# First products of the out-projection put into a chunk's last Strassen tile, side products later, zero products gone, stores by pairs

## The chip, the cores and the metric

The kernel runs on one core of one Trainium2 chip. The metric is device time in microseconds (us) from the first to the last instruction of a run; lower is better. Engine names are those of the profile: PE (TensorE matmuls), PEld (its weight loads), DVE (VectorE), ACT (ScalarE), POOL (GpSimd) and SP (SyncE, which issues most DMAs). A line number such as L751 is a line of the kernel before.

## The reference, cut to what matters

A decoder trunk of two layers over 512 tokens and 16 meta tokens, width 1024, all in float32. Each layer is FFN, token mixer, FFN, and each of these is wrapped in two RMSNorms:

```python
h = h + 0.5 * rmsnorm(swiglu(rmsnorm(h, g[0]), w_ffn_in[layer, 0], w_ffn_out[layer, 0]), g[1])
hn = rmsnorm(h, g[2])
mix = gla_mixer(...) if layer < 1 else swa_mixer(...)   # gated linear attention, then sliding-window attention
h = h + rmsnorm(mix, g[3])
h = h + 0.5 * rmsnorm(swiglu(rmsnorm(h, g[4]), w_ffn_in[layer, 1], w_ffn_out[layer, 1]), g[5])

def swiglu(x, w_in, w_out):
    gate, up = jnp.split(x @ w_in, 2, axis=-1)          # 2 x 2816 columns
    return (jax.nn.silu(gate) * up) @ w_out
```

So there are four FFNs. Between the layers one shared key/value set is computed. The output is `h` without the meta tokens.

## The kernel before, in words

**Numbers.** Every float32 factor of a large product is split into a high and a low part in a format that PE runs fast (`float32r`), and a product is three matmuls: high by high, low by high, high by low (`mm3s`, L333). ACT makes the high part (a copy) and DVE the low part (a subtraction), for activations and for weights alike; weights are split as they arrive (`split_part` L224, `split_pair` L236).

**An FFN** (`ffn`, L604) has 22 hidden tiles of 128, in chunks of 4, 6, 6 and 6 (`FF_CHUNKS`). A chunk makes its hidden tiles and then runs its part of the out-projection, which adds into `Y`. The first chunk (`ci == 0`) uses plain products: `x_first` (L509) multiplies two groups of tokens (the second, `gi == 1`, waits for less of the norm), then `x_units` (L486). Where a group has at most 256 columns, `x_first` puts two results into one bank of PSUM, and clears the bank first with a matmul of zeros by zeros over 512 columns. During that chunk `right_factors` (L666) prepares the right factors of the Strassen products on ACT and DVE.

The other three chunks of an FFN, 12 in all, go by `Strassen` (L711). A tile has seven products of 12 matmuls: `head` (11), `body` (s1, s2, 12, s3) and `tail` (s4, 22). Between them ACT and DVE copy and add. What matters here is in `body`:

```python
self.product(t.a, t, "s2", "t2", False)
act.activation(t.u2, t.a, AF.Copy)                  # L751
self.product(self.d, t, "12", "21", False)
act.activation(t.g1, self.d, AF.Silu)
self.product(t.a, t, "s3", "t3", False)             # adds to t.a, so it waits for L751
```

For all but the last tile, the head of the next tile stands between body and tail. After the tail, `gated` (L769) makes the hidden tile: a gate product on DVE (L770, L771), the high part on ACT (L774) and the low part on DVE (L775). The hidden tile of a tile is therefore finished while PE is already in the body of the next one.

**The out-projection** (`out_proj`, L552) has a unit for each of 8 output tiles `m` and each group of tokens: six hidden tiles by three matmuls, into one bank, which DVE adds to `Y` (L572). Groups are 272 and 256 columns wide in layer 0 and 512 in layer 1; in the last chunk of an FFN the units go by the two halves (`split_groups`), so that the norm of the first half can start early. `flow.wait(*jobs)` ahead of it makes sure that the instructions of all `gated` jobs have been emitted.

**Norms.** Sums of squares are made on ACT and POOL; PE adds them over partitions (`st_` matmuls), a chain of small instructions on DVE or POOL takes the inverse root (`rstd`, L348), and PE spreads the result over partitions (`r_` matmuls).

**What sets the order.** Each engine runs its instructions in the order in which the Python program emits them. The main loops emit PE's matmuls; side work (splits, norms, attention cores) is a generator in `Flow` (L60). Every matmul moves `flow.clock` on by its estimated time, and `flow.pump` runs those generators whose time has come; a `yield` of a number puts the rest off by so much, so an `st_` or `r_` matmul comes into PE's order a set time after the work that it needs was emitted. PE waits wherever that time was too short. Weights are loaded and split ahead under a budget (`set_ahead`, `prefetch` L300, `cap`).

**The end.** `Residual.store` (L471) adds the last residual by pairs of tiles, DVE and POOL, and stores each tile with a DMA of its own from SP.

Of the kernel before, what the change touches and what calls it, by code (L numbers as in the profile page):

```python
# [43 lines left out]
SCORE = 0.8  # L44
STAGGER = 5.0
SOFT = 5.0
NORM = 3.0
LAG = 3
NEG = -1e30
# [74 lines left out]
def trunk_kernel(ctx: ExitStack, tc, a, out):  # L124
# [19 lines left out]
    def ps(name):  # L144
        return pp.tile([P, 512], F32, tag="ps", name=name)
# [184 lines left out]
        released[0] += n  # L330


    def mm3s(outs, j, x, g, start, stop, shared=False):  # L333
        t, n = g
        cols = slice(j % 4 * P, (j % 4 + 1) * P)
        xh, xl = x[:, 0, t : t + n], x[:, 1, t : t + n]
        for o, w in outs:
            mm(o, w[j // 4][:, 0, cols], xh, start and not shared, False)
            mm(o, w[j // 4][:, 1, cols], xh, False, False)
        for i, (o, w) in enumerate(outs):  # L340
            mm(o, w[j // 4][:, 0, cols], xl, False, stop and (not shared or i % 2 == 1))
            flow.pump()

    def mm3(o, w, j, x, g, start, stop):
        mm3s([(o, w)], j, x, g, start, stop)


    def rstd(sq, n, dim, half, name, eng=pool):  # L348
        c = 128 if n % 128 == 0 else n // 4
        nch = n // c  # L350
        st = ps(f"st_{name}")
        for j in range(nch):
            for i, t in enumerate(sq):
                mm(st[:c, j : j + 1], t[:, j * c : (j + 1) * c], ones[:, 0:1], i == 0, i == len(sq) - 1)
        av = sm.tile([P, 4], F32, tag="av", name=f"av_{name}")
        yv = sm.tile([P, 4], F32, tag="yv", name=f"yv_{name}")
        zv = sm.tile([P, 4], F32, tag="zv", name=f"zv_{name}")
        wv = sm.tile([P, 4], F32, tag="wv", name=f"wv_{name}")
        aa, yy, zz, ww = av[:c, :nch], yv[:c, :nch], zv[:c, :nch], wv[:c, :nch]
        if eng is dve:  # L360
            dve.tensor_scalar(aa, st[:c, :nch], 1.0 / dim, 1e-6, op0=ALU.mult, op1=ALU.add)
        else:
            act.activation(aa, st[:c, :nch], AF.Identity, scale=1.0 / dim, bias=eps[:c])
        eng.tensor_scalar(yy.bitcast(I32), aa.bitcast(I32), -0.5, RSQRT_MAGIC, op0=ALU.mult, op1=ALU.add)

        eng.tensor_tensor(zz, yy, yy, op=ALU.mult)
        eng.tensor_tensor(zz, zz, aa, op=ALU.mult)
        eng.tensor_scalar(ww, zz, 0.375, -1.25, op0=ALU.mult, op1=ALU.add)
        eng.tensor_tensor(ww, ww, zz, op=ALU.mult)
        if eng is dve:  # L370
            dve.scalar_tensor_tensor(yy, ww, 1.875, yy, op0=ALU.add, op1=ALU.mult)
            dve.tensor_tensor(zz, yy, yy, op=ALU.mult)
# [10 lines left out]
        eng.tensor_tensor(  # L383
            dg[:c, :n].rearrange("p (j c) -> p j c", c=c),
            (hident if half else ident)[:c, :c].unsqueeze(1).to_broadcast([c, nch, c]),
            yy.unsqueeze(2).to_broadcast([c, nch, c]),
            op=ALU.mult,
        )
        yield DCHAIN if eng is dve else CHAIN
        r = ps(f"r_{name}")  # L390
        mm(r[:, :n], ones[:c, :], dg[:c, :n])
        return r
# [17 lines left out]
    class Operand:  # L410
# [25 lines left out]
        def factors(self, gi, eng=pool):  # L436
# [1 line left out]
                self.rt = sm.tile([P, TOK], F32, tag="R", name=f"R_{self.name}", bufs=2)  # L438
            o, n = self.groups[gi]
            yield FACT  # L440
            r = yield from rstd(self.accs[gi], n, D, False, f"{self.name}_{o}", eng)
            act.activation(self.rt[:, o : o + n], r[:, :n], AF.Copy)

        def need(self, gi, k):
# [3 lines left out]
    class Residual:  # L448
# [4 lines left out]
        def run(self, gi, g, sums):  # L453
# [7 lines left out]
            for k in range(KD):  # L461
# [4 lines left out]
                nxt.build(gi, k)  # L466
                nxt.sumsq(gi, k)
                yield 1.0
            nxt.rjob[gi] = flow.spawn(nxt.factors(gi))

        def store(self, gi, g, r):  # L471
            o, n = g
            rb = r[:, :n].unsqueeze(1).to_broadcast([P, 2, n])
            for k in range(0, KD, 2):
# [3 lines left out]
                t = t.rearrange("p (k n) -> p k n", n=n)  # L478
                dve.tensor_tensor(t, y, rb, op=ALU.mult)
                (pool if last else dve).tensor_tensor(h, t, h, op=ALU.add)  # L480
                for j in (k, k + 1):
                    sp.dma_start(out[j, :, o - META : o - META + n], H[:, j, o : o + n])
                yield 1.0


# [23 lines left out]
    def x_first(x, nu, evac, opening=False, behind=(), first_ahead=8):  # L509
# [13 lines left out]
        for gi, some in order + [(1, both)]:  # L523
# [4 lines left out]
            shared = n <= 256  # L528
            if shared:
                banks = [ps(f"x{used[0]}_{i}_{gi}") for i in some[::2]]  # L530
                for b in banks:
                    mm(b.rearrange("p (a c) -> p a c", c=P), zeros, zeros.unsqueeze(1).to_broadcast([P, 4, P]), True, False)
                pst = [banks[i // 2][:, i % 2 * 256 : i % 2 * 256 + n] for i in range(len(some))]
            else:
                pst = [ps(f"x{used[0]}_{i}_{gi}")[:, :n] for i in some]
# [13 lines left out]

    def out_proj(hid, groups, split_groups, first, finish=None, tailm=0, packed=False):  # L552
        nh = len(hid)
        ws = []

        def tile_of(m, j):
# [2 lines left out]
                ws.append(next_w())  # L559
            return ws[i], c  # L560

        def unit(m, g):
            o, n = g
            p = ps(f"y{used[0]}_{m}_{o}")
            for j, t in enumerate(hid):
                w, c = tile_of(m, j)
                mm3(p[:, :n], w, c, t, g, j == 0, j == nh - 1)
            y = Y[:, m, o : o + n]
            if first:
                act.activation(y, p[:, :n], AF.Copy)  # L570
# [12 lines left out]
            return (m + 1) * nh // 8 if packed else m + 1  # L583

        freed = 0
        for m in range(KD - tailm):
            for g in groups:
                unit(m, g)
# [15 lines left out]
    def ffn(x, groups, finish, opening=False, tail=4):  # L604
# [31 lines left out]
        for ci, (lo, hi) in enumerate(FF_CHUNKS):  # L636
# [9 lines left out]
            else:  # L646
# [2 lines left out]
                tiles = Strassen(z, halves)  # L649
                cur = tiles.head(new_hid())  # L650
                while cur:
                    tiles.body(cur)
                    nxt = tiles.head(new_hid()) if len(hids) < hi - lo else None
                    jobs.append(tiles.tail(cur, nxt is None))
                    cur = nxt
            flow.wait(*jobs)
            if lo < LAST:
                out_proj(hids, groups, x.groups, ci == 0)
            else:
                set_ahead(32)  # L660
                cap[0] = min(used[0] + NLAST + tail, len(units))
                out_proj(hids, groups, x.groups, False, finish, KD, True)

# [47 lines left out]
    class Strassen:  # L711
# [32 lines left out]
            act.activation(self.d, t.a, AF.Copy)  # L744
            return t

        def body(self, t):
# [3 lines left out]
            act.activation(t.u2, t.a, AF.Copy)  # L751
# [30 lines left out]
    def gla(x, finish):  # L782
        set_ahead(10)
        with tc.tile_pool(name="gp", bufs=1) as gp:
# [61 lines left out]
            def core(h, before):  # L846
# [516 lines left out]
```

## Time and profile before

| | |
|---|---|
| time, median of 3 runs (range) | 1956.11 us (1955.54 to 1958.57) |
| time of the profiled execution | 1955.57 us |
| span of its trace | 1953.7 us |
| PE busy | 1893.7 us, 97% |
| PEld, DVE, ACT, POOL busy | 92%, 73%, 51%, 11% |
| DMA moved | 174.63 MB, mean 89 GB/s |

The span runs from the first to the last instruction. "Busy" of PE counts modelled ends of pipelined matmuls, so PE's real pace is read from the starts: the time of a run of equal matmuls, divided by their number. In the list of waits a row names the waiting engine, the tile that it writes and its line, then what released it, and then the sum, the number of times and the longest, in us. In a table of windows each engine's busy time stands with its number of instructions in brackets, and PEclk is the granted TensorE clock as a share of full speed.

### The profile page before, as it was taken

Reading aid. Unit: us, or ns where it says so; the run is one execution under the profiler, and the core shown is the slowest. Engines: PE = TensorE matmul, PEld = TensorE weight load, DVE = VectorE, ACT = ScalarE, POOL = GpSimd, SP = SyncE. Lnnn points to the kernel's source line nnn. Section 1 sums busy time; section 2 is a strip of 40 time slices with the busy share of each in tenths; the row PEclk is TensorE's granted clock in tenths of the full one; section 3 lists DMA queues with packets and bytes.
Section 4 is the critical chain, followed back from the end, with each engine's and each line's share of the span. In section 5 each row is a group of like instructions: output and inputs, shape, how many; then the busy total and the mean of one; then the engine's idle time right before and its main releaser. Section 6 shows DMA issues by size and latency. Waiting matters only on the chain.

```text
span 1953.7 us, 37401 instructions
## 1 busy us (share of the span) xinstructions
PE 1893.7 (97%) x14522; PEld 1802.5 (92%) x14522; DVE 1420.8 (73%) x2868; ACT 1002.2 (51%) x2268; POOL 214.9 (11%) x417
## 2 busy tenths in 40 slices
PE   8999999999999999999999999999998999999997
PEld 7999999999999999999999898989976898989897
DVE  7885858665464788585887776768779779858584
ACT  5663636653235555353574453535636665636363
POOL 2000000221121400000024000000252140000002
PEclk9999999999999999999999999999999999999999
DMA  4332333322113122333251123232411212333331
GB/s 161 96 102 90 102 94 108 110 66 65 55 45 119 55 71 86 104 90 106 93 172 50 55 89 117 82 114 93 136 57 42 72 49 71 98 102 109 97 109 44
DMA packets 102145, 174.63 MB, mean 89 GB/s; under 512 B 11472, under 2 KB 24272, under 8 KB 101968
## 3 DMA queue, kind: packets, MB, share of 16 engines
q1 hardware_dynamic: 101680, 172.11, 28.3%
q8 instruction: 114, 1.87, 0.4%
q14 instruction: 63, 0.52, 0.1%
q10 hardware_dynamic: 288, 0.13, 0.0%
HBM read 170.10 MB, written 2.10 MB: 88 GB/s over the span
## 4 chain that ended last, share of the span: by engine, by line
PE 71%; DVE 20%; ACT 6%; issue 3%; POOL 0%; DMA 0%; SPq 0%; DVEq 0%; ACTq 0%
PE y L162 30%; PE x L162 16%; PE a L162 11%; DVE raw L251 4%; PE c L162 4%; DVE w_s L246 3%; DVE w L246 3%; ACT w_s L245 3%; PE d L162 3%; DVE w L227 2%; PE o L162 1%; PE e L162 1%; PE po L162 1%; ACT w L226 1%; DVE hidl0f L775 1%
## 5 line engine op out<-in xcount | busy, mean ns | idle before, releaser
L246 DVE TENSOR_TENSOR w_s<-raw,w_s 128x512 fp32r<-128x512 f32 x288 | 194.0, 690 | 134.6 <-ACT w_s L245 132.4
L227 DVE TENSOR_TENSOR w<-raw,w 128x512 fp32r<-128x512 f32 x378 | 244.0, 671 | 34.3 <-ACT w L226 32.4
L162 PE MATMUL y<-hidl0f,w 128*128 128x256 f32 (+1 forms) x2112 | 261.7, 285 | 1.3 <-DVE hidl0f L408 0.5
L162 PEld LDWEIGHTS y<-hidl0f,w 128*128 128x128 f32 x2112 | 258.8, 188 | 3.0 <-DVE hidl0f L408 1.0
L162 PE MATMUL y<-hidl1f,w 128*128 128x512 f32 (+1 forms) x1344 | 251.1, 346 | 1.5 <-ACT hidl1f L407 1.0
L245 ACT ACTIVATE w_s<-raw 128x512 fp32r<-128x512 f32 x288 | 175.4, 628 | 146.5 <-DVE raw L251 143.2
L162 PEld LDWEIGHTS y<-hidl1f,w 128*128 128x128 f32 x1344 | 212.3, 188 | 37.8 <-ACT hidl1f L407 1.8
L226 ACT ACTIVATE w<-raw 128x512 fp32r<-128x512 f32 x378 | 209.2, 586 | 51.3 <-PE y L162 41.8
L403 POOL TENSOR_TENSOR acc_post<-acc_post,sq_post 128x256 f32<-128x256 f32 (+1 forms) x72 | 57.0, 791 | 1408.8 <-ACT sq_post L402 1408.6
L251 DVE TENSOR_TENSOR raw<-raw,raw 128x512 f32<-128x512 f32 x288 | 197.9, 687 | 5.5
L246 DVE TENSOR_TENSOR w<-raw,w 128x512 fp32r<-128x512 f32 x216 | 148.2, 687 | 41.1 <-ACT w L245 40.2
L162 PE MATMUL x<-x_l0m,w 128*128 128x272 f32 (+1 forms) x1200 | 159.9, 290 | 0.0
L245 ACT ACTIVATE w<-raw 128x512 fp32r<-128x512 f32 x216 | 133.8, 621 | 47.9 <-PE y L162 47.6
L162 PEld LDWEIGHTS x<-x_l0m,w 128*128 128x128 f32 x1200 | 150.9, 190 | 1.2
L572 DVE TENSOR_TENSOR Y<-y,Y 128x256 f32<-128x256 f32 (+2 forms) x176 | 83.2, 473 | 80.7 <-PE y L162 80.2
L162 PE MATMUL a<-zl0f_t,w_s 128*128 128x264 f32 x864 | 118.7, 287 | 8.5 <-ACT c L751 8.5
L162 PE MATMUL a<-zl1f_t,w_s 128*128 128x256 f32 x864 | 115.1, 282 | 8.7 <-ACT c L751 8.4
L162 PEld LDWEIGHTS a<-zl0f_t,w_s 128*128 128x128 f32 x864 | 110.9, 190 | 9.8 <-ACT c L751 9.8
L162 PEld LDWEIGHTS a<-zl1f_t,w_s 128*128 128x128 f32 x864 | 107.0, 188 | 11.1 <-ACT c L751 11.1
L162 PE MATMUL x<-x_l0f,w 128*128 128x256 f32 (+1 forms) x768 | 102.2, 293 | 7.3 <-ACT w L226 6.4
L162 PEld LDWEIGHTS x<-x_l0f,w 128*128 128x128 f32 x768 | 98.7, 195 | 8.9 <-ACT w L226 6.7
L162 PE MATMUL x<-x_l1f,w 128*128 128x256 f32 (+1 forms) x576 | 93.2, 320 | 0.5 <-DVE x_l1f L426 0.5
(485 smaller groups left out, 3299.6 us busy)
## 6 DMA issues: line engine op xcount, KB each, us to landing
raw<-in_w_in SPq DMA_DIRECT2D x352, 256.0 KB, 2.9
raw<-in_w_out SPq DMA_DIRECT2D x96, 256.0 KB, 3.5
raw<-in_gla_in SPq DMA_DIRECT2D x50, 256.0 KB, 3.1
raw<-in_w_last SPq DMA_DIRECT2D x48, 256.0 KB, 3.1
raw<-in_w_out SPq DMA_DIRECT2D x64, 128.0 KB, 3.0
raw<-in_gla_out SPq DMA_DIRECT2D x16, 256.0 KB, 2.7
raw<-in_w_q SPq DMA_DIRECT2D x16, 256.0 KB, 3.9
raw<-in_swa_out SPq DMA_DIRECT2D x16, 256.0 KB, 2.7
```

Source lines behind the costliest of these rows:

```text
L162: inst = pe.matmul(o, lhs, rhs, start=start, stop=stop, skip_group_check=onto)
L226: act.activation(w[:, 0, :m], raw[:, :m], AF.Copy)
L227: dve.tensor_tensor(w[:, 1, :m], raw[:, :m], w[:, 0, :m].bitcast(F32), op=ALU.subtract)
L245: act.activation(w[:, 0, :512], src, AF.Copy)
L246: dve.tensor_tensor(w[:, 1, :512], src, w[:, 0, :512].bitcast(F32), op=ALU.subtract)
L251: dve.tensor_tensor(dst, dst, src, op=ALU.add)
L403: pool.tensor_tensor(sums[0][:, :n], sums[0][:, :n], t[:, :n], op=ALU.add)
L572: dve.tensor_tensor(y, p[:, :n], y, op=ALU.add)
L775: dve.scalar_tensor_tensor(t.hid[:, 1, g], t.h, -1.0, t.hid[:, 0, g].bitcast(F32), op0=ALU.mult, op1=ALU.subtract)
```

## The change

1. `out_proj` is now a generator, `out_steps`, behind a wrapper of the old name. A unit can be begun early: `begin(m, g)` does the products with all hidden tiles but the last, and `unit` later adds the last one. In a Strassen chunk the first unit is begun inside the last tile's body, between the product `12` and the product `s3` (`between`); after the tail, one further unit (512 columns) or two (256 and 272) are begun before `flow.wait(*jobs)`.
2. `BEHIND = 2.2` is added to the put-off times of some side products: the second group's `st_` (spawn of `factors`) and, in the opening, its `r_`; the transposes of the first attention core (`STATE_KEYS`); the `r_` of the last core's norm in `gla` (`h // 3`).
3. `x_first` has no zero matmuls: the first product of a shared bank has `start`, and those of the second half of the bank have not. That is 2 matmuls fewer in each of the first stages of the FFNs and mixers with two groups of 272 and 256 columns, 4 fewer where both groups have 256; 20 in all.
4. `store` issues one DMA for a pair of tiles, and two of the last four go from ACT instead of SP.

```diff
+BEHIND = 2.2
@@ mm3s
-        for o, w in outs:
-            mm(o, w[j // 4][:, 0, cols], xh, start and not shared, False)
-            mm(o, w[j // 4][:, 1, cols], xh, False, False)
         for i, (o, w) in enumerate(outs):
-            mm(o, w[j // 4][:, 0, cols], xl, False, stop and (not shared or i % 2 == 1))
+            second = shared and i % 2 == 1
+            mm(o, w[j // 4][:, 0, cols], xh, start and not second, False, second)
+            mm(o, w[j // 4][:, 1, cols], xh, False, False, second)
+        for i, (o, w) in enumerate(outs):
+            second = shared and i % 2 == 1
+            mm(o, w[j // 4][:, 0, cols], xl, False, stop, second)
             flow.pump()
@@ rstd(..., more=0.0)
-        yield DCHAIN if eng is dve else CHAIN
+        yield (DCHAIN if eng is dve else CHAIN) + more
@@ Operand.factors
-            r = yield from rstd(self.accs[gi], n, D, False, f"{self.name}_{o}", eng)
+            r = yield from rstd(self.accs[gi], n, D, False, f"{self.name}_{o}", eng, gi * BEHIND if eng is dve else 0.0)
@@ Residual.run
-            nxt.rjob[gi] = flow.spawn(nxt.factors(gi))
+            nxt.rjob[gi] = flow.spawn(nxt.factors(gi), gi * BEHIND)
@@ Residual.store
-                for j in (k, k + 1):
-                    sp.dma_start(out[j, :, o - META : o - META + n], H[:, j, o : o + n])
+                to = out[k : k + 2, :, o - META : o - META + n].rearrange("k p n -> p k n")
+                (act if gi and k % 4 else sp).dma_start(to, h)
@@ x_first
-                for b in banks:
-                    mm(b.rearrange("p (a c) -> p a c", c=P), zeros, zeros.unsqueeze(1).to_broadcast([P, 4, P]), True, False)
@@ out_proj
-    def out_proj(hid, groups, split_groups, first, finish=None, tailm=0, packed=False):
+    def out_proj(*args, **named):
+        for _ in out_steps(*args, **named):
+            pass
+
+    def out_steps(hid, groups, split_groups, first, finish=None, tailm=0, packed=False, jobs=()):
...
+        begun = {}
+
+        def begin(m, g):
+            o, n = g
+            p = begun[m, o] = ps(f"y{used[0]}_{m}_{o}")
+            for j, t in enumerate(hid[:-1]):
+                w, c = tile_of(m, j)
+                mm3(p[:, :n], w, c, t, g, j == 0, False)
+
         def unit(m, g):
             o, n = g
-            p = ps(f"y{used[0]}_{m}_{o}")
-            for j, t in enumerate(hid):
-                w, c = tile_of(m, j)
-                mm3(p[:, :n], w, c, t, g, j == 0, j == nh - 1)
+            if (m, o) not in begun:
+                begin(m, g)
+            p = begun[m, o]
+            w, c = tile_of(m, nh - 1)
+            mm3(p[:, :n], w, c, hid[-1], g, nh == 1, True)
...
+        if jobs:
+            order = [(m, g) for m in range(KD - tailm) for g in groups]
+            order += [(m, split_groups[0]) for m in range(KD - tailm, KD)]
+            begin(*order[0])
+            yield
+            for m, g in order[1 : 2 if order[1][1][1] == SEQ else 3]:
+                begin(m, g)
+            flow.wait(*jobs)
@@ ffn, a Strassen chunk
-                    tiles.body(cur)
-                    nxt = tiles.head(new_hid()) if len(hids) < hi - lo else None
-                    jobs.append(tiles.tail(cur, nxt is None))
+                    last = len(hids) == hi - lo
+                    if last:
+                        fin = (finish, KD, True) if lo >= LAST else (None, 0, False)
+                        proj = out_steps(hids, groups, x.groups, False, *fin, jobs)
+                        end = used[0] + NLAST + tail
+                    tiles.body(cur, (lambda: next(proj)) if last else (lambda: None))
+                    nxt = None if last else tiles.head(new_hid())
+                    jobs.append(tiles.tail(cur, last))
                     cur = nxt
...
+            for _ in proj:
+                pass
@@ Strassen.body(t, between)
             self.product(self.d, t, "12", "21", False)
             act.activation(t.g1, self.d, AF.Silu)
+            between()
             self.product(t.a, t, "s3", "t3", False)
@@ gla, core and its norm
-                yield STATE_KEYS
+                yield STATE_KEYS + (0 if h else BEHIND)
...
-                    r = yield from rstd(accs[gi], n, 256, True, f"go{h}_{gi}")
+                    r = yield from rstd(accs[gi], n, 256, True, f"go{h}_{gi}", more=h // 3 * BEHIND)
```

More of the change, by code (lines that the diff above doesn't have):

```diff
@@ L345, in mm3, with rstd @@
         mm3s([(o, w)], j, x, g, start, stop)
-    def rstd(sq, n, dim, half, name, eng=pool):
+    def rstd(sq, n, dim, half, name, eng=pool, more=0.0):
         c = 128 if n % 128 == 0 else n // 4
@@ L651, in ffn @@
                 while cur:
-                    tiles.body(cur)
-                    nxt = tiles.head(new_hid()) if len(hids) < hi - lo else None
-                    jobs.append(tiles.tail(cur, nxt is None))
-                    cur = nxt
[L656 to L659, printed above, removed]
+                    last = len(hids) == hi - lo
[6 more added lines that the diff above has]
+                    jobs.append(tiles.tail(cur, last))
+                    cur = nxt
+            if ci == 0:
+                flow.wait(*jobs)
+                out_proj(hids, groups, x.groups, True)
+                continue
+            if lo >= LAST:
                 set_ahead(32)
-                cap[0] = min(used[0] + NLAST + tail, len(units))
-                out_proj(hids, groups, x.groups, False, finish, KD, True)
+                cap[0] = min(end, len(units))
+            for _ in proj:
+                pass
     def right_factors(x, halves, z, plain):
@@ L745, in head, with body @@
             return t
-        def body(self, t):
+        def body(self, t, between):
             self.product(t.c, t, "s1", "t1", True)
```

## The prediction

> **What bounds the kernel now.** I read the page's chain and its groups first, then the list of PE's waits, then the stretches around them.
>
> ```profile
> PE 71%; DVE 20%; ACT 6%; issue 3%; POOL 0%; DMA 0%; SPq 0%; DVEq 0%; ACTq 0%
> ...
> L227 DVE TENSOR_TENSOR w<-raw,w 128x512 fp32r<-128x512 f32 x378 | 244.0, 671 | 34.3 <-ACT w L226 32.4
> ```
>
> PE carries 71% of the chain that ends last, DVE and ACT 26%, DMA nothing; the second row gives the price of a weight split on DVE, 0.67 us. So time is to be had where PE waits for DVE or ACT, or where it does needless matmuls. The waits:
>
> ```profile
> PE a L162 <- ACT c L751: 16.9, 12, 1.8
> ...
> PE pk L174 <- DVE f L880: 2.1, 1, 2.1
> PE st_l0f L162 <- ACT acc_l0f L399: 2.0, 1, 2.0
> PE r_l0f L162 <- DVE dg_l0f L383: 1.6, 2, 1.3
> PE r_go L162 <- POOL dg_go L383: 1.6, 1, 1.6
> ...
> PE st_l1m L162 <- POOL acc_l1m L403: 1.1, 1, 1.1
> PE st_kv L162 <- ACT acc_kv L399: 1.1, 1, 1.1
> PE st_l1m L162 <- ACT acc_l1m L399: 1.0, 1, 1.0
> ```
>
> The first row has 12 waits, as many as there are Strassen chunks. They are the s3 product of each chunk's last tile. The second chunk shows it (the last number of the second row is the wait):
>
> ```profile
> 143.23 1.61 PE L162 MATMUL d<-zl0f,w 128*128 128x264 f32 x12
> 146.10 1.74 PE L162 MATMUL a<-zl0f_t,w_s 128*128 128x264 f32 x12 [1.26 <-ACT c L751]
> ...
> 150.62 3.57 PE L162 MATMUL y<-hidl0f,w 128*128 128x272 f32 x27
> ```
>
> The copy it waits for comes late because ACT's order puts the hidden tile of the tile before (L774) ahead of it, and that waits for DVE:
>
> ```profile
> 144.33 0.65 ACT L774 ACTIVATE hidl0f<-c 128x528 fp32r<-128x528 f32 x1 [0.76 <-DVE c L771]
> ...
> 145.67 0.38 ACT L751 ACTIVATE c<-a 128x264 f32<-128x264 f32 x1
> ```
>
> The pace of PE comes from long runs of equal matmuls in the chain in order of time:
>
> ```profile
> 150.78 35.27 PE y L162 x288
> ...
> 1190.90 30.31 PE y L162 x129
> ```
>
> That is 0.122 us for 272 or 256 columns (35.27/288) and 0.235 us for 512 (30.31/129).
>
> **1. Products put into the last tile.** In the order of instructions of the changed program, 15 matmuls (five hidden tiles by three) move from the start of the out-projection to the place between the d product and s3; none is added. ACT's order around L751 stays. The d product's 12 matmuls take 12 x 0.122 = 1.46 us from 143.23, to 144.69, so PE really stands still for 1.41 us before 146.10, where the row says 1.26 (it lets a matmul end later). With 0.14 us more for each, the 12 waits are 16.9 + 1.7 = 18.6 us. The cover is 15 x 0.122 = 1.83 us, or 15 x 0.235 = 3.53 us in layer 1's 512-column chunks; the longest wait is 1.8 + 0.14 = 1.94 us.
>
> The products bring a wait of their own: the last three need the hidden tile of the tile before, the low part (L775) at the fifteenth matmul. Here are that instruction in this chunk and in the last one, with the product that follows:
>
> ```profile
> 145.01 0.71 DVE L775 SCALAR_TENSOR_TENSOR hidl0f<-c,hidl0f 128x528 fp32r<-128x528 f32 x1
> ```
>
> ```profile
> 1898.48 0.68 DVE L775 SCALAR_TENSOR_TENSOR hidl1f<-c,hidl1f 128x512 fp32r<-128x512 f32 x1
> ...
> 1899.16 1.69 PE L162 MATMUL a<-zl1f_t,w_s 128*128 128x256 f32 x12 [1.72 <-ACT c L751]
> ```
>
> In the first it is done at 145.72, and the fifteenth matmul starts at 144.69 + 14 x 0.122 = 146.40: no wait. In the last chunk the d product ends at 1899.16 - 1.72 - 0.14 = 1897.30, the fifteenth would start at 1899.01, and L775 ends at 1899.16. I leave 0.25 us there, and the same in the last chunk of each of the other FFNs, which end like it: 4 x 0.25 = 1.0 us. Queued behind these products in PE's order are s3, s4 and 22 and so the last hidden tile; s3 starts up to 3.53 - 1.41 = 2.1 us later than now in the 512-column chunks. DVE's addition behind s3 (L755) holds weight splits behind it by as much; the out-projection's first weights are split ahead of it, since the d product's own weights are later in DVE's order.
>
> After the tail PE has 30 begun matmuls as cover (3.7 us), or 15 of 512 columns (3.5 us), where it now has 15. The hidden tile is late by less than that today: PE goes from 150.62 through the first 15 without a wait that the list shows. I take nothing for it.
>
> **2. The clock.** Stretches of lower granted clock stand right behind waits that the change goes for. The longest wait for L751, and a table of windows (PEclk is the third column from the end):
>
> ```profile
> 343.31 2.72 PE L162 MATMUL a<-zl0f_t,w_s 128*128 128x264 f32 x12 [1.80 <-ACT c L751]
> ```
>
> ```profile
> 343.70:347.10 3.40, 3.40 (x18) 3.40 (x17) 2.63 (x6) 2.43 (x6) 0.00 (x0) 0.50 0.88 254
> 347.10:350.50 3.40, 3.40 (x30) 3.40 (x29) 2.40 (x5) 0.58 (x2) 0.00 (x0) 1.00 0.78 248
> 442.70:446.10 3.40, 3.40 (x18) 3.40 (x17) 2.00 (x5) 3.17 (x7) 0.00 (x0) 0.50 0.32 89
> 674.80:678.20 3.40, 3.40 (x19) 3.40 (x17) 1.86 (x4) 1.04 (x2) 2.65 (x9) 0.50 0.83 216
> 1899.20:1902.60 3.40, 3.40 (x29) 3.40 (x30) 3.33 (x7) 2.89 (x6) 0.00 (x0) 1.00 0.65 214
> ```
>
> The three at 0.50 follow the 1.8 us wait for L751, the 2.1 us for `pk` and the 2.0 us for `st_l0f`. Each does 18 or 19 matmuls where a full stretch does 30: 11 or 12 x 3.4/30, 1.3 us. With the waits I let them go: 1.3 us in part 1 and 2.6 us in part 3. The Trainium skill, in "TensorE: Matmul & The Clock Gate", Part 1, has the array fall to half rate after an idle window of about 3.4 us, and its closing table warns of gaps over about 3 us. By that rule these waits would cost no clock and the sum below would be 3.9 us smaller. The trace disagrees: half clock begins here behind waits of 1.8 to 2.1 us, so I go by the rows.
>
> Part 1 is thus 18.6 - 1.0 + 1.3 = **18.9 us** (bounds 0, if the wait for L775 took its place, and 19.9).
>
> **3. Side products later, and no zeros.** The 20 zero matmuls over 512 columns are 20 x 0.235 = 4.7 us of PE. `BEHIND` moves an `st_` or `r_` 2.2 us by the program's clock, about the size of each wait. But what follows an `st_` (the inverse root, the scaling by DVE) starts no earlier in real time. PE gets ahead and keeps the gain only if DVE isn't the bound up to PE's next need of it:
>
> ```profile
> 40.00:65.00 25.00, 24.53 (x196) 24.06 (x196) 23.75 (x49) 11.52 (x26) 0.00 (x0) 1.00 0.22 64
> 674.00:705.00 31.00, 30.48 (x235) 29.98 (x234) 24.84 (x51) 11.56 (x28) 3.84 (x12) 0.94 0.24 69
> 1052.00:1105.00 53.00, 52.50 (x339) 47.35 (x338) 37.87 (x79) 17.54 (x36) 7.62 (x16) 1.00 0.16 50
> 1441.00:1490.00 49.00, 42.09 (x246) 28.85 (x246) 41.11 (x116) 26.38 (x105) 19.15 (x28) 0.97 0.20 65
> ```
>
> DVE is the third engine in each row (PE, PEld, DVE, ACT, POOL): 95%, 80%, 71% and 84% busy. By stage, gross and what I keep:
>
> - First FFN: `r_l0f` 1.6 and 2 zeros 0.5 = 2.1. DVE is busy 23.75 of 25 us up to the hidden tile that the out-projection needs; its order has one right-factor instruction fewer ahead of it, about a weight split's 0.67 us. Kept 0.5.
> - GLA: 2 zeros 0.5, `pk` 2.1, its clock 1.3, `r_go` 1.6 = 5.5; PE bounds this stage. Kept 5.1.
> - Second FFN: 2.0, clock 1.3, 2 zeros 0.5 = 3.8. DVE's order has four right-factor instructions fewer ahead of the last hidden tile, 4 x 0.67 = 2.7 us. Kept 2.6.
> - Key/value and third FFN: `st_kv` 1.1 and 6 zeros 1.4 = 2.5; DVE has room. Kept 2.2.
> - Sliding-window attention: `st_l1m` 2.1 and 4 zeros 0.9 = 3.0. DVE bounds the softmax stretch, and 12 projection matmuls that fill PE's waits there now come earlier. Kept 1.2, between a loss of those 12 x 0.235 = 2.8 and a gain of 3.0.
> - Fourth FFN: 4 zeros 0.9. Kept 0.5.
>
> Gross 17.8, kept **12.1 us**.
>
> **4. Stores.** The last eight stores are issued over 4 us:
>
> ```profile
> 1947.32 4.01 SPq L482 DMA_DIRECT2D out<-H  x8
> 1947.66 1.28 DVE L480 TENSOR_TENSOR H<-t_out,H 128x512 f32<-128x512 f32 x2
> ```
>
> The last sum is ready at 1948.94 and the last issue ends at 1951.33. Four issues on two queues could save half of these 2.4 us, or nothing if the transfers themselves take the time; no row shows a 256 KB store. I take **0.6 us**, the middle of 0 and 1.2. What is queued on ACT behind them is nothing.
>
> **Sum:** 18.9 + 12.1 + 0.6 = 31.6 us off the profiled execution's 1955.57 gives 1924.0; the median of the runs is 0.5 us above that execution, so **1924.5 us**.
>
> **The rivals.**
>
> - *All of it is kept* (DVE's slack suffices everywhere, no wait left in part 1): 19.9 + 17.8 + 1.2 = 38.9 us, 1917.2. For it: DVE has 5 to 29% of room in the four stretches. Against: 23.75 of 25. Chance 0.12.
> - *DVE takes the side gains*: only GLA's 5.1 stays, and attention loses 2.8: 18.9 + 2.3 + 0.6 = 21.8 us, 1934.3. For it: the 95% and the 84%. Against: fewer right-factor instructions ahead of the hidden tiles. 0.15.
> - *Half-clock stretches come at other places*, behind waits that stay: 3.9 us less, 1928.4. For it: the 1.72 us wait at 1899.16 has none behind it (last row of that table), 1.8 us has, so place decides too. 0.10. By the rule of the Trainium skill's "TensorE: Matmul & The Clock Gate", Part 1, the time would be this one as well.
> - *It doesn't do what it says*: the products in the tile wait for L775 as long as s3 does for L751, part 1 is 0: 12.7 us, 1943.4. Against: L775 at 145.72. 0.03.
> - *Slower*: s3's delay is passed to DVE through L755, and out-projection splits of 0.67 us each come ahead of the last hidden tile, so that it outlasts the units begun. From 31.6/12 = 2.6 us, four splits, in each chunk it decides; with six (4.0 us) the kernel is 12 x 4.0 - 31.6 = 16.4 us slower, 1956.1 + 16.4 = 1972.5. Against: DVE's order has no split moved there. 0.04.
>
> The forecast itself (1919 to 1928) has 0.56.
>
> **How the numbers follow.** Range 1915 to 1936: it holds the forecast, the first three rivals but for their ends, about 0.85. A measurement of this kernel tells about 0.2%, 4 us, from no change. Faster by more than that: all cases but the slower one, 0.96, less 0.02 for mixtures of the last two that end near zero; so 0.94, 0.02 within, 0.04 slower.
>
> **What would show it.** Right: the row of waits for L751 falls from 12 times to at most the few of 0.2 us; `y` rows stand between d and s3; `st_l0f`, `st_l1m`, `st_kv`, `pk`, `r_go` are gone from the list; half-clock stretches at most one before the end; 20 matmuls fewer. Wrong: a row of `y` waiting for L775 or L774 of over 2 us in all, a wait of `y` for the plain chunk's hidden tiles (L407, L408) that grows by what `st_` and `r_` gave up, or longer waits of `ptm` and `sc` in attention.

## The result, and the profile after

| | before | changed |
|---|---|---|
| median of 4 runs each, same chip (range) | 1957.34 us (1955.54 to 1959.47) | 1932.53 us (1931.28 to 1935.86) |
| profiled execution, its span | 1955.57, 1953.7 us | 1932.53, 1930.5 us |
| PE instructions | 14522 | 14502 |

The ratio is 0.9875, with a 95% interval of 0.9858 to 0.9893: 24.8 us faster by the medians, 23.2 us by the spans of the two profiles, where 31.6 were forecast. The time is 8 us above the forecast and inside its range. That agreement is in part luck: it hides two errors of opposite sign, 4.2 and 12.6 us, as the stages will show.

In the changed kernel lines from L162 on lie further down: matmuls are L163, the copy L751 is L784, the low part L775 is L809, L407 and L408 are L411 and L412. First its chain of work and its list of PE's waits (sum, times, longest, in us):

```profile
PE 82%; DVE 12%; ACT 3%; issue 2%; POOL 1%; DMA 0%; SPq 0%; DVEq 0%; ACTq 0%
```

```profile
...
PE ptm L175 <- DVE mt L1169: 5.3, 2, 3.5
PE r_go L163 <- POOL dg_go L387: 4.1, 3, 2.4
PE y L163 <- ACT hidl0f L411: 3.1, 2, 2.5
...
PE o L163 <- DVE pt L1190: 1.7, 1, 1.7
...
PE x L163 <- ACT x_l1m L429: 1.3, 1, 1.3
PE o L163 <- DVE pt L1191: 1.1, 1, 1.1
...
PE x L163 <- DVE x_l1m L430: 0.6, 1, 0.6
...
PE a L163 <- ACT c L784: 0.2, 1, 0.2
```

PE's share of the chain rose from 71 to 82%: the last row, 16.9 us in 12 waits before, is nearly empty. `st_l0f`, `st_l1m`, `st_kv` and `pk` are gone from the list. In their place stand waits that were not there or were smaller: `r_go` 4.1 (from 1.6), `y` for the plain hidden tiles 3.1 (from 0.5), `x` for `x_l1m` 1.9 and `o` for `pt` 2.8 (neither stood in the list of before). The second chunk's last tile shows the first gain; the fifteen `y` matmuls stand between d and s3, and nothing waits:

```profile
144.84 1.62 PE L163 MATMUL d<-zl0f,w 128*128 128x264 f32 x12
146.29 2.05 PE L163 MATMUL y<-hidl0f,w 128*128 128x272 f32 x15
148.18 1.63 PE L163 MATMUL a<-zl0f_t,w_s 128*128 128x264 f32 x12
```

The next table is what the study rests on. It cuts each profile at the start of a matmul that every kernel has (the first of a Strassen chunk, the first `st_post_` of a stage) and gives the length of each stretch, for other kernels as the difference from before. In brackets stand the half-clock stretches of 3.413 us that begin in it. The kernels are described with their runs below; "again" is a second profile of the changed kernel.

| stretch | forecast | before | changed | again | p1_only | behind0 | best | between_only | ahead_only |
|---|---|---|---|---|---|---|---|---|---|
| up to the first chunk | -0.5 | 87.40 (0) | +1.74 (2) | -1.10 (0) | -0.03 (0) | -1.73 (0) | -0.09 (1) | -0.41 (0) | -0.55 (0) |
| chunks 1 to 3 | | 282.93 (1) | -7.13 (0) | -7.14 (0) | -7.09 (0) | -6.88 (0) | -6.91 (0) | +1.56 (1) | -0.57 (1) |
| GLA | -5.1 | 264.04 (1) | -1.18 (0) | +0.39 (1) | -1.47 (0) | -1.68 (0) | -0.03 (1) | -1.43 (0) | +0.11 (1) |
| second FFN, plain chunk | -2.6 | 92.64 (1) | -3.57 (0) | -3.63 (0) | +0.07 (1) | -0.82 (1) | -3.70 (0) | +1.62 (2) | +0.07 (1) |
| chunks 4 to 6 | | 281.24 (0) | -5.00 (0) | -5.03 (0) | -5.21 (0) | -5.24 (0) | -5.11 (0) | +1.67 (0) | -0.60 (0) |
| key/value, third FFN, plain chunk | -2.2 | 117.55 (0) | -1.91 (0) | -1.75 (0) | +1.60 (1) | +0.60 (1) | -1.92 (0) | +1.48 (1) | +0.03 (0) |
| chunks 7 to 9 | | 272.70 (0) | -6.36 (0) | -6.35 (0) | -6.15 (0) | -6.15 (0) | -6.34 (0) | +1.86 (1) | -1.55 (0) |
| attention | -1.2 | 169.79 (1) | +6.32 (4) | +6.30 (4) | +2.16 (3) | +1.53 (2) | +1.36 (2) | +1.64 (2) | +1.48 (2) |
| fourth FFN, plain chunk | -0.5 | 83.92 (0) | -1.07 (0) | -1.04 (0) | +0.10 (0) | -0.33 (0) | -1.10 (0) | -0.01 (0) | -0.06 (0) |
| chunks 10 to 12 | | 271.52 (0) | -4.62 (0) | -4.75 (0) | -5.24 (0) | -5.37 (0) | -4.84 (0) | +3.19 (1) | +1.00 (1) |
| end | -0.6 | 30.01 (3) | -0.47 (4) | -0.48 (3) | +0.26 (4) | -0.48 (3) | -0.87 (3) | +0.23 (4) | +0.17 (3) |
| the 12 chunks together | -18.9 | | -23.11 | -23.27 | -23.69 | -23.64 | -23.20 | +8.28 | -1.72 |

The chunks gained 23.1 us, 4.2 more than forecast. The rest of the program, where 12.7 were forecast, gained 0.1 (1.3 in the second profile).

### The profile page after: what moved, and what is told of

Its sections match the earlier page's. It is cut to its first block, busy times and chain, and to the rows that moved or that the text cites. A ratio compares the mean times of both kernels' runs of the same rounds, so it can differ in the third digit from the quotient of the medians.

```text
span 1930.5 us, 37342 instructions
## 1 busy us (share of the span) xinstructions
PE 1889.1 (98%) x14502; PEld 1801.1 (93%) x14502; DVE 1419.5 (74%) x2868; ACT 1002.5 (52%) x2268; POOL 223.0 (12%) x417
## 4 chain that ended last, share of the span: by engine, by line
PE 82%; DVE 12%; ACT 3%; issue 2%; POOL 1%; DMA 0%; SPq 0%; DVEq 0%; ACTq 0%
PE y L163 30%; PE a L163 18%; PE x L163 14%; PE c L163 8%; PE d L163 4%; DVE raw L252 1%; DVE w L228 1%; ACT w_s L246 1%; DVE w_s L247 1%; DVE w L247 1%; PE e L163 1%; PE o L163 1%; PE po L163 1%; DVE xsl0f L723 0%; PE ps L163 0%
## 5 line engine op out<-in xcount | busy, mean ns | idle before, releaser
L163 PE MATMUL y<-hidl0f,w 128*128 128x272 f32 (+1 forms) x2112 | 264.8, 287 | 3.3 <-ACT hidl0f L411 3.1
L163 PEld LDWEIGHTS y<-hidl0f,w 128*128 128x128 f32 x2112 | 261.7, 190 | 4.4 <-ACT hidl0f L411 3.5
L163 PE MATMUL y<-hidl1f,w 128*128 128x512 f32 (+1 forms) x1344 | 251.1, 346 | 1.7 <-ACT hidl1f L411 1.4
L163 PEld LDWEIGHTS y<-hidl1f,w 128*128 128x128 f32 x1344 | 212.3, 188 | 36.6 <-ACT hidl1f L411 2.3
L407 POOL TENSOR_TENSOR acc_post<-acc_post,sq_post 128x256 f32<-128x256 f32 (+1 forms) x72 | 59.1, 821 | 1376.7 <-ACT sq_post L406 1376.1
L163 PE MATMUL x<-x_l0m,w 128*128 128x272 f32 (+1 forms) x1200 | 158.1, 288 | 0.0
L163 PEld LDWEIGHTS x<-x_l0m,w 128*128 128x128 f32 x1200 | 149.3, 189 | 1.1
L163 PE MATMUL a<-zl0f_t,w_s 128*128 128x264 f32 x864 | 117.3, 285 | 0.0
L163 PE MATMUL a<-zl1f_t,w_s 128*128 128x256 f32 x864 | 114.5, 281 | 0.3 <-ACT c L784 0.2
L163 PEld LDWEIGHTS a<-zl0f_t,w_s 128*128 128x128 f32 x864 | 110.1, 188 | 0.2
L163 PEld LDWEIGHTS a<-zl1f_t,w_s 128*128 128x128 f32 x864 | 107.3, 188 | 1.9 <-ACT c L784 1.5
L163 PE MATMUL x<-x_l0f,w 128*128 128x256 f32 (+1 forms) x768 | 100.4, 291 | 7.2 <-ACT w L227 5.8
L163 PEld LDWEIGHTS x<-x_l0f,w 128*128 128x128 f32 x768 | 97.0, 192 | 8.5 <-ACT w L227 5.8
L163 PE MATMUL x<-x_l1f,w 128*128 128x256 f32 (+1 forms) x576 | 92.7, 320 | 0.0
```

The source lines that it names most:

```text
L163: inst = pe.matmul(o, lhs, rhs, start=start, stop=stop, skip_group_check=onto)
L407: pool.tensor_tensor(sums[0][:, :n], sums[0][:, :n], t[:, :n], op=ALU.add)
```

## The experiments

Three theories to begin with. **A**: part 1 makes nearly all of the gain; putting side products off only moves the waits. **B**: each part gains what the prediction says by itself, and they spoil each other only together. **C**: part 1 brings 10 to 14 us, and the rest comes from the side products. The first four kernels split the change; before ran at 1957.89 us beside them.

**p1_only.** The changed kernel with `BEHIND = 0.0`, the zero matmuls and the old stores: part 1 alone.

> The kernel before with part 1 alone (products put into the last tile; zeros, put-off times and stores as before). Theory A (part 1 brings nearly all of the gain, the side edits about nothing in sum, because their waits only move and new half-clock stretches come behind them): 20 to 24 us faster than before, 1933 to 1937 us, at most 4 us from the changed kernel. Theory B (each part gains by itself what the prediction says, and they get in each other's way only together): 18.9 us faster, about 1938, and the side edits alone gain 12. Theory C (part 1 brings less than predicted, the rest comes from the side edits): 10 to 14 us faster, 1943 to 1947.

1937.38 us, ratio 0.9894 (0.9881 to 0.9908): 20.5 us faster, 18.0 to 23.3 by the interval. C falls. A (20 to 24 us) and B (18.9 us) both lie inside, so this run doesn't tell them apart. By the profiles its chunks gained 23.7 us, and outside them this kernel is 2.7 us longer than before; two rows of the table, key/value and attention, gained half-clock stretches there.

**rest_only.** The changed kernel without part 1:

```diff
-            begin(*order[0])
-            yield
-            for m, g in order[1 : 2 if order[1][1][1] == SEQ else 3]:
-                begin(m, g)
             flow.wait(*jobs)
+            yield
-                    tiles.body(cur, (lambda: next(proj)) if last else (lambda: None))
+                    tiles.body(cur, lambda: None)
```

> The changed kernel without part 1 (side products later, no zeros, stores by pairs). Theory A: within 4 us of the kernel before, 1953 to 1961. Theory B: 12.7 us faster, about 1944. Theory C: 10 to 13 us faster, 1944 to 1947. A and B differ too in the attention stage: A sees there the waits of x for x_l1m with a half-clock stretch behind them here too, B does not.

1960.86 us, ratio 1.0013 (1.0004 to 1.0022). This is not clean: as in the changed kernel, the last chunk of an FFN reads further weights ahead (`set_ahead(32)`) before it waits for the hidden tiles, but here no begun products cover that. The list of waits shows it at the hidden tiles of those four chunks, where before has 0.5 us for the low part and none for the high part:

```profile
PE y L163 <- ACT hidl1f L805: 2.1, 2, 1.1
...
PE y L163 <- ACT hidl0f L805: 0.9, 2, 0.5
```

Its chunks are 6.3 us longer than before (+0.59, +1.11, +2.91, +1.73), one half-clock stretch more among it. Without them the rest is 5.24 - 6.34 = 1.1 us shorter than before by the profiles, where 12.7 were forecast. A holds on that reading, and B falls; the attention stage, +4.91 with 2 half-clock stretches, loses here too, without part 1.

**behind0.** The changed kernel with `BEHIND = 0.0`.

> The changed kernel with BEHIND = 0 (part 1, no zeros, new stores, put-off times as before). Theory A: the waits for st_l0f, st_l1m, st_kv, pk and r_go come back (some 8 us with their clock) and the waits that grew in the changed kernel shrink by as much: within 4 us of the changed kernel. Theory B: 7 to 9 us slower than the changed kernel (the part of the 12.1 us that is not zeros), about 1940. If the put-off times do harm where PE has nothing else to do (first FFN, attention), some us faster than the changed kernel.

1930.34 us, ratio 0.9862 (0.9849 to 0.9874): at or below the changed kernel (0.9875 and, in a later set of runs, 0.9880; the intervals overlap), where B has 7 to 9 us more. The put-off times, 13.1 of the 17.8 us gross in the forecast (all but the zeros' 4.7), brought nothing together. Beside p1_only, on the same chip, it is 7.0 us faster by the medians and 5.6 by the spans of the profiles: the zeros (4.7 us of PE), the stores, and in the profiles one half-clock stretch fewer ahead of the end.

**zeros_back.** The changed kernel with the zero matmuls.

> The changed kernel with the 20 zero matmuls back (20 x 0.235 = 4.7 us of PE). Theory A: PE only waits less behind them, for x_l1m and ptm above all, and the half-clock stretch at 1418 may go: between 4 us faster and 1 us slower than the changed kernel. Theory B: 3 to 4.7 us slower.

1936.35 us, ratio 0.9891 (0.9877 to 0.9905), 3.8 us slower than the changed kernel by the medians; these are from two sets of runs, and the intervals overlap. With behind0 against p1_only it speaks for B's number, and this point of A falls: without the zeros PE saves time even here.

The stage table says where the put-off times help and where they harm, and that the half-clock stretches differ between kernels that are the same up to that place. So the next four, beside before at 1958.09:

**after_again.** The changed kernel, profiled once more.

> The changed kernel unchanged, a second profile. The half-clock stretches of six profiles so far start on a grid of 3.413 us in each, and the grid lies at another place after the start in each. Theory G (a grid window of 3.413 us in which PE stands still for about 2.1 us or more gives half clock in the next one, and the grid runs freely): waits of 1.2 to 2.7 us stand where they stood, but the half-clock stretches come behind other ones of them (behind the 3.7 us of ptm in any case), again on a grid of its own. Theory P (the place in the program decides): the stretches are at 63, 1418 and 1452 us again, within 1 us. Time 1930 to 1936 us by both.

1932.61 us, ratio 0.9880 (0.9865 to 0.9895). The half-clock stretches in attention began again within 1 us of their places (1417.5 and 1451.6 us; G expected it of the second alone), but those of the opening were gone and one stood at 540 us, which P excludes. So theory G, on the whole. Here are the waits in the opening and the windows around them, of the changed kernel first (the columns of a window: its time and length, then PE, PEld, DVE, ACT and POOL busy, PEclk, DMA share, GB/s):

```profile
63.80 6.42 PE L163 MATMUL y<-hidl0f,w 128*128 128x272 f32 x26 [2.46 <-ACT hidl0f L411]
```

```profile
59.84:63.25 3.41, 1.50 (x13) 1.28 (x11) 3.41 (x8) 1.16 (x3) 0.00 (x0) 1.00 0.41 142
63.25:66.67 3.42, 2.87 (x11) 2.58 (x12) 3.42 (x8) 3.35 (x8) 0.00 (x0) 0.50 0.12 32
66.67:70.08 3.41, 3.41 (x18) 3.41 (x17) 3.41 (x7) 1.69 (x4) 0.00 (x0) 0.50 0.87 255
```

And of the second profile:

```profile
63.40 0.52 PE L163 MATMUL y<-hidl0f,w 128*128 128x272 f32 x2 [2.45 <-ACT hidl0f L411]
```

```profile
58.98:62.39 3.41, 1.97 (x16) 1.75 (x15) 3.41 (x7) 1.62 (x4) 0.00 (x0) 1.00 0.49 154
62.39:65.80 3.41, 2.13 (x15) 1.91 (x16) 3.41 (x9) 2.88 (x7) 0.00 (x0) 1.00 0.01 4
65.80:69.22 3.42, 3.42 (x30) 3.42 (x29) 3.42 (x6) 2.82 (x7) 0.00 (x0) 1.00 0.88 256
536.84:540.26 3.42, 1.01 (x5) 0.42 (x4) 0.43 (x1) 0.21 (x1) 3.26 (x14) 1.00 0.01 2
540.26:543.67 3.41, 3.29 (x14) 2.95 (x14) 1.85 (x3) 0.60 (x1) 0.12 (x1) 0.50 0.00 0
```

The same wait, 2.46 and 2.45 us. In the first profile most of it fell into one window of the grid, PE was busy for 1.50 us in it, and the clock was halved for the next two windows. In the second the edge of the window cut the wait in two, and nothing followed; instead the `r_go` wait at 540 was halved, which in the first profile was not. The first chunk began 2.84 us apart (+1.74 and -1.10) in one and the same program.

**no_open.** `rstd(..., eng)` in `Operand.factors`, without the put-off `r_`.

> The changed kernel without the put-off r_ in the opening. Theory S: the wait of y for hidl0f (2.5 us) shrinks to some 0.5, r_l0f waits 1.3 again, and the first Strassen chunk begins 2 to 3.5 us sooner; 1929 to 1931 us. Rival: DVE is the bound up to there whatever PE's order (95% busy), the hidden tile is ready at the same time, and only the waits change their names: same as the changed kernel within 1 us.

1930.01 us, ratio 0.9869 (0.9853 to 0.9884). The opening is 1.78 us shorter than before, 0.68 shorter than in the second profile; `y` waits 0.8 us for the hidden tile and `r_l0f` 1.3. So the put-off `r_` did cost, but 0.7 us, a quarter of what S expected; the rest of the 3.5 us to the first profile goes with its two half-clock stretches. The two whole times can't be told apart.

**no_l1m.** The put-off is left out for the norm ahead of attention:

```diff
-            nxt.rjob[gi] = flow.spawn(nxt.factors(gi), gi * BEHIND)
+            nxt.rjob[gi] = flow.spawn(nxt.factors(gi), gi * BEHIND * (nxt.name in ("l0m", "l0f1", "kv", "l1f1")))
```

> The changed kernel with the st_ of the attention stage where it was before (name l1m). Theory S: st_l1m waits 2 to 3 us again, the waits of x for x_l1m (1.9 us) and of o for pt (2.8 us) go, and from the first x of that stage to the last y 1.5 to 5 us are gained, of which up to 3.4 us are half clock: 1928 to 1931 us. Rival: DVE bounds the stage; the stage keeps its length within 1 us, 1931 to 1934 us.

1927.35 us, ratio 0.9851 (0.9837 to 0.9865). The attention stage is 1.92 us longer than before (3 half-clock stretches) where the changed kernel's is 6.30 (4): 4.4 us gained, and 5.3 by the medians, beside after_again. S holds. PE's waits from 1405 to 1580 us, of the second profile of the changed kernel, and then of this one:

```profile
PE ptm L175 <- DVE mt L1169: 5.2, 2, 3.5
PE o L163 <- DVE pt L1190: 1.7, 1, 1.7
PE sc L163 <- DVE Y L1151: 1.3, 1, 1.3
PE x L163 <- ACT x_l1m L429: 1.3, 1, 1.3
PE o L163 <- DVE pt L1191: 1.1, 1, 1.1
PE sc L163 <- DVE so L412: 0.7, 1, 0.7
PE x L163 <- DVE x_l1m L430: 0.6, 1, 0.6
```

```profile
PE ptm L175 <- DVE mt L1169: 4.7, 2, 3.2
PE st_l1m L163 <- POOL acc_l1m L407: 3.0, 1, 3.0
PE sc L163 <- DVE pt L1191: 1.4, 1, 1.4
PE sc L163 <- DVE q L1035: 1.3, 1, 1.3
PE sc L163 <- DVE Y L1151: 0.8, 1, 0.8
```

Both lists come to about the same (11.9 and 11.2 us), so the 4.4 us can't be read from the sum of the waits. The put-off turned one wait of 3.0 us ahead of the softmax into waits for the operand's tiles (1.9) and, later, for the softmax itself.

**best.** The put-off only for the second FFN, the key/value stage and the fourth FFN (`l0f1`, `kv`, `l1f1`), none in the opening, for `pk`, for `r_go` and for `l0m`, `l1m`.

> The changed kernel with BEHIND kept only for the second FFN, the key/value stage and the fourth FFN (names l0f1, kv, l1f1), where its stages were shorter than with BEHIND = 0 by 3.0, 2.5 and 0.7 us. Theory S (the put-off times help where PE bounds the stage and harm where the work behind the norm does): these gains add up and nothing else changes, 5 to 6 us less than with BEHIND = 0: ratio to before about 0.983, 1924 us. Theory N (a gain in one stage is lost in the next one): the same as with BEHIND = 0 within 2 us, 0.986.

1925.97 us (1924.36 to 1926.92), ratio 0.9844 (0.983 to 0.9858). It beats both kernels: 6.6 us under the changed kernel beside it, 32.1 under before. Against behind0 the three stages are shorter by 2.9, 2.5 and 0.8 us, as S has it. In the first two, behind0 has a half-clock stretch each and best has none, so about 3 of the 6.2 us are clock. It isn't all chance: the stretch of the second FFN stands in all six kernels that wait for `st_l0f` there, that of the key/value stage in four of the six without the put-off, and none stands in any of the eight profiles with it. By the whole spans 3.0 us are left, since one more half-clock stretch fell into the opening (+1.64) and one into GLA (+1.65). The medians are 4.4 us apart, from two sets of runs, and the intervals overlap.

The last four ran beside before at 1958.08.

**between_only.** p1_only, but only the 15 matmuls in the tile; the two lines that begin further units ahead of `flow.wait(*jobs)` are left out.

> The kernel before with the first half of part 1 alone: the 15 matmuls between the d product and s3, no unit begun ahead of the wait for the jobs. If the 15 matmuls are what hides the copy L751: the 12 waits go and the Strassen chunks gain 22 to 24 us together, as with the whole of part 1 (23.7), 1936 to 1939 us. If the later units are needed as cover for the last hidden tile: waits of y for the hidden tile (L774, L775) of 0.5 us or more in each chunk, 5 to 10 us less gain.

1967.02 us, ratio 1.0046 (1.0033 to 1.0059): 8.9 us *slower* than before. The second guess holds, and by far more than it said. The second chunk's last tile and the list of waits:

```profile
144.26 2.05 PE L163 MATMUL y<-hidl0f,w 128*128 128x272 f32 x15
146.15 1.62 PE L163 MATMUL a<-zl0f_t,w_s 128*128 128x264 f32 x12
147.60 1.62 PE L163 MATMUL e<-zl0f,w_s 128*128 128x264 f32 x12
149.06 1.63 PE L163 MATMUL a<-zl0f_t,w 128*128 128x264 f32 x12
151.89 0.51 PE L163 MATMUL y<-hidl0f,w 128*128 128x272 f32 x2 [1.20 <-ACT hidl0f L806]
```

```profile
PE y L163 <- ACT hidl1f L806: 9.7, 6, 2.5
PE y L163 <- ACT hidl0f L806: 9.5, 6, 2.4
```

The wait for L751 is gone, and 12 waits for the last hidden tile, 19.2 us, took its place: the fifteen products had been the cover behind the tail. By the starts these waits are 21.2 us, only 2.3 more than the 18.9 that went; 8 half-clock stretches ahead of the end, against 4 before, go with much of the rest. In the four last chunks the earlier weight read-ahead named under rest_only is in these waits too (2.5 us instead of 1.4 by the starts). The eight other chunks, free of it, are 1.4 us longer than before together, where p1_only's are 13.3 shorter.

**ahead_only.** p1_only, but all units begun after the tail, none in the tile.

> The kernel before with the second half of part 1 alone: the first units begun after the tail and ahead of the wait for the jobs, nothing between d and s3. If the 15 matmuls in the tile do the work: the 12 waits for L751 stay at 16.9 us, and the time is that of before within 3 us, less at most the 1.4 us that y waits for the low part L775 in four chunks. If the cover after the tail does: 5 to 10 us faster.

1955.95 us, ratio 0.9986 (0.9976 to 0.9996). The wait for L751 stays, 17.1 us in 12, as the first guess had it. So one half of part 1 loses 8.9 us, the other gains 2.1, and together they gain 20.5.

**best_pk.** best with `yield STATE_KEYS + (0 if h else BEHIND)` back.

> The kernel called best, with the transposes of the first attention core put off as in the changed kernel (pk). Theory M (a wait for a chain on DVE and POOL only moves: PE gets ahead and waits at the next product that needs the chain): the pk wait of 2.1 us goes, r_go waits for one to three heads more, by about 2 us together, and the GLA stage keeps its length within 1 us but for half clock: 1924 to 1928 us. The prediction's view (PE bounds this stage): 2.1 us shorter, or 3.8 where a half-clock stretch stood behind pk, and r_go waits no longer than in best.

1929.35 us, ratio 0.9853 (0.984 to 0.9867); best was 0.9844, from another set of runs, and the intervals overlap. The waits of best, then of this kernel:

```profile
PE pk L175 <- DVE f L914: 2.1, 1, 2.1
PE r_go L163 <- POOL dg_go L387: 1.8, 1, 1.8
```

```profile
PE r_go L163 <- POOL dg_go L387: 5.8, 5, 1.6
...
PE pk L175 <- DVE f L914: 0.2, 1, 0.2
```

1.9 us left `pk` and 4.0 came to `r_go`. GLA is 3.03 us longer than before, best's 0.03 shorter, each with one half-clock stretch. M has it that the wait only moves, and the prediction that it goes; here the stage became 3.1 us longer.

**zeros_only.** before without the zero matmuls, in the form of rest_only.

> The kernel before without the 20 zero matmuls and nothing else. If the zeros are PE time wherever they stand (20 x 0.235 = 4.7 us): 3.5 to 5 us faster, ratio about 0.9978. If, as the prediction has it, they are kept where PE bounds the stage and lost where DVE does: 0.5 in GLA, 1.4 in key/value and third FFN, 0.5 in each of the other FFNs at most, nothing in attention: about 3 us. If they come to nothing without part 1: within 1.5 us of before.

1959.36 us, ratio 1.0012 (1.0001 to 1.0023). This run does not answer its question: the same read-ahead ahead of uncovered hidden tiles lengthens its chunks by 4.7 us (and one half-clock stretch is among them). Without the chunks it is 0.9 us shorter than before, with two half-clock stretches more ahead of the end. In attention the four zeros' 0.9 us stand as a longer wait for `st_l1m` (3.1 us, from 2.1). What the zeros are worth is better read from behind0 and zeros_back.

## Why the prediction was right and wrong

**Part 1** (18.9 forecast, 23.1 by the profile, 20.5 alone by the medians) was right in its mechanism. Added up from the starts of the matmuls, as the prediction does it, the 12 waits were 18.9 us (18.6 forecast). The clock behind the longest was worth more than the 1.3 us counted by matmuls: the third chunk gained 3.8 us for a wait of 1.97, so 1.8 more. Of the 1.0 us kept for L775, 0.6 was needed: by the starts, `y` in the tile waits 0.28 and 0.30 us for it in the last chunks of the third and fourth FFN, and not in those of the first two. The remaining 2.4 us is 0.2 a chunk, of which waits of 0.15 to 0.4 us (for L751 in other tiles, for the hidden tile: 3.2 us together before, 1.7 after, these 0.6 among them) explain 1.5; the rest stays unexplained. One sentence was right for a thin reason: "I take nothing for it", on the cover after the tail. between_only and ahead_only show that neither half gains much alone: the hidden tile comes when it comes, and PE saves the wait in the tile only if it has other work behind the tail.

**Side products** were wrong, and this is the failed step: "Side products later, and no zeros", kept 12.1. By the table the six stages kept nothing: they lost 0.3 us (+1.74 - 1.18 - 3.57 - 1.91 + 6.32 - 1.07 = +0.33) in the first profile and gained 0.8 in the second. Point by point:

- *Second FFN* 3.6 (2.6), *key/value and third FFN* 1.9 (2.2), *fourth FFN* 1.1 (0.5): right. In best these keep 3.7, 1.9 and 1.1.
- *GLA* 1.2 (5.1). "PE bounds this stage" failed. Its 1.18 us is less than one half-clock stretch, which before has there and the changed kernel has not. At an equal number of stretches the put-offs together make the stage 0.3 to 0.5 us longer: with none, changed -1.18 against p1_only -1.47 and behind0 -1.68; with one, the second profile +0.39 against best -0.03. best_pk puts off `pk` alone, and there the PE time saved is waited for at `r_go`, with interest. Why `r_go` lost more than `pk` gave, and why the changed kernel with its other put-offs does not lose these 3.1 us, was not tried.
- *Attention* lost 6.3 (gain of 1.2 forecast, bounds -2.8 to 3.0): outside the bounds. The 12 projection matmuls did come out of the softmax stretch. Before and changed, the last of them:

```profile
1492.77 2.34 PE L162 MATMUL x<-x_l1m,w 128*128 128x512 f32 x9
...
1497.87 2.34 PE L162 MATMUL x<-x_l1m,w 128*128 128x512 f32 x9
```

```profile
1470.20 0.95 PE L163 MATMUL x<-x_l1m,w 128*128 128x512 f32 x3
...
1474.32 1.64 PE L163 MATMUL x<-x_l1m,w 128*128 128x512 f32 x6
```

  The 18 that stood at the end, in two blocks of nine, have become the 6 of the last row, and the waits of `o` for `pt`, 2.8 us, are new. no_l1m shows that the put-off of `l1m` is the cause of 4.4 us, one half-clock stretch among them. Kernels with equal numbers of stretches in this stage divide it further:

| attention, us against before | 2 half-clock stretches | 4 |
|---|---|---|
| `l1m` not put off | behind0 +1.53, best +1.36 | best_pk +3.79 |
| `l1m` put off | rest_only +4.91, no_open +4.83 | changed +6.32, again +6.30 |

  So the put-off by itself costs 2.5 to 3.5 us, about the bound of 2.8. The other 3 us of the 6.3 go with the clock, which the bound left out: four half-clock stretches instead of one. The zeros gained hardly anything to set against it: behind0 and best, without them, are 1.4 to 1.5 us longer than before with one stretch more.
- *First FFN* lost 1.7 in the one profile and gained 1.1 in the other (0.5 forecast). The wait of `y` for L411 grew to 2.5 us, as "What would show it" lists under wrong.

**The clock.** "With the waits I let them go" held for the stretches behind L751 and `st_l0f`, and failed as a sum, because others came in the opening and in attention. Ahead of the end the changed kernel has 6 half-clock stretches (5 in the second profile) where before has 4. The rival "half-clock stretches come at other places" named it, at 3.9 us and a chance of 0.10; the rival "DVE takes the side gains" (1934.3 us) came nearest to the time and was right on attention. Its GLA part was wrong too.

**Stores** 0.5 us (0.6): the end is 0.7 us shorter than in p1_only, which has the old stores.

## What to carry to other kernels

A wait that is filled with work taken from behind it is only gained if something else covers the place that the work came from; look for both before counting either. Putting a side product off in an in-order queue helps where the engine itself bounds the stage up to the next product that needs the same chain; elsewhere the wait comes back there, often larger. Judge it stage by stage from the starts of the same matmuls in both traces: here three places gained 6.2 us, about 3 of it clock, and the others gave it all back.

## What the runs showed of the hardware

**Half clock is decided on a grid.** In each of the 14 profiles all half-clock stretches begin at multiples of 3.413 us from one another (before: 343.70, 442.69, 674.79, 1473.51; the first two are 29 x 3.4133 apart), and where the grid lies after the start differs from execution to execution. For each window of that grid at full clock, from 20 us on, I added up by how much the starts of successive matmuls lie further apart than the median for their shape:

| PE stands still in the window | windows | next one at half clock |
|---|---|---|
| 0.9 to 2.0 us | 269 | 14 |
| 2.0 to 2.2 us | 25 | 16 |
| over 2.2 us | 44 | 44 |

With other cut-offs for what counts as standing still the first two rows shift (the first from 262 to 327 windows, 13 to 21 of them); that every window over 2.2 us has half clock behind it stays. So a wait of about 2 us costs some 1.7 us more or nothing, by where the grid happens to lie in that execution, and by this count one of 4.4 us or more would always cost it (2 x 2.2, if the edge halves it). That the window of 3413 ns runs freely is in the Trainium skill, "TensorE: Matmul & The Clock Gate", Part 1, and these traces agree. It speaks of an idle window as the condition; here 2.2 of 3.41 us were enough in all cases seen. For a forecast, a wait of 2 us is thus priced with a chance, not by the place where one profile shows its stretch, and lengths of a stage in two profiles are compared below some 2 us only with their stretches counted.
